# Forget gates' running sums: from 8 partitions x 1024 tokens to 128 partitions x 64 tokens

## The chip, the core and the metric

The kernel runs on one core of a Trainium2 chip. The core has five engines that each work through a queue of their own in order: TensorE (PE, with weight loads shown as PEld), VectorE (DVE), ScalarE (ACT), GpSimd (POOL) and SyncE (SP), which here only starts DMA transfers. ACT and POOL start transfers too. The engines wait for each other by semaphores. The metric is the device time of one execution in microseconds (us), as the median of several runs.

## The reference

One layer of a hybrid encoder: a normalisation, one wide projection, two kinds of attention, an output projection, and a feed-forward part. The change is about one small piece, the forget gates of the first attention:

```
log_f = jax.nn.log_sigmoid((fa + forget_bias).astype(jnp.float32))   # 8 heads x 1024 tokens
c = jnp.cumsum(log_f, axis=-1)                                        # running sum over the tokens
sc = q k^T * scale + c[query] - c[key]                                # used as a bias of the scores
```

`fa` is eight columns of the projection (one per head). So of each head 1024 numbers are needed: z = fa + bias, log sigmoid(z) = min(z, 0) - log(1 + exp(-|z|)), and the running sum of that over the tokens.

## The kernel before

The activations lie transposed, 1024 features on partitions by two halves (h = 0, 1) of 512 tokens. Matrix products are done in float32 quality with pairs of fp32r parts, a high part and a low part (`wh`, `wl` of a weight, `...h`, `...l` of an operand), three PE instructions for each. The projections use a Strassen scheme: a unit computes 2x2 blocks in seven products of 12 matmuls each, named here by their operands: B11, T2, T1, T3, B21, B22, T4. Four PSUM banks (`u_0` to `u_3`) belong to a unit. After a product DVE or ACT reads its bank (`p` on ACT L543; `u` L545, `c` L547 and L549, `cc` L557 on DVE), and the later products B22 and T4 add into banks 2 and 3 after `c` has read them. PSUM has two pools of four banks, `psd[0]` and `psd[1]`, which the units take in turn.

The order of work around the change is that of lines 608 to 616: `project_qk(0)`; then for each of four steps `project_v(i)`, `project_qk(i+1)` and `finish()`, which transposes the projected v through PE (`vtp`, L594) into banks of `psd[1]` and splits it (`vs`, L278; casts on ACT, subtractions on DVE). `forget()` is called once, behind the first of these steps. A scheduler of the framework sorts the recorded instructions into each engine's queue, by its own estimate of when each can start; so the instructions of `forget` are mixed into those of the second v unit and the second and third q/k units. POOL splits the weights (`wl`, L167, and the sums `S`); SP loads them (`wr`, L160, four buffers); ACT casts the high parts (`wh`, L165) and sends every output of a q/k unit with six DMA issues (L573, L574).

`forget` (L407) works in two halves of 512 tokens on 8 partitions, one per head. For each half it loads the raw columns from `c_dram` (where L385 had put them), multiplies by rstd, and does ten more DVE instructions and two ACT functions (Exp L418, Ln L420, each with a load of its table); the running sum is a scan (L428) that starts from the last value of the half before. The sums go back to `c_dram` (L432). They are read at the start of attention (`cr`, L438, and `bc`, L453).

Of the kernel before, what the change touches and what calls it, by code (L numbers as in the profile page):

```python
# [11 lines left out]
F32 = mybir.dt.float32  # L12
F32R = mybir.dt.float32r
AF = mybir.ActivationFunctionType
ALU = mybir.AluOpType
# [62 lines left out]
def hs(h):  # L78
    return slice(h * HALF, (h + 1) * HALF)
# [3 lines left out]
def hybrid_block(ctx: ExitStack, tc: tile.TileContext, xT, xN, g1, wall, wf, fb, relb, relt, rows, g2, g3, outT):  # L83
# [28 lines left out]
    def tmp(name, dt=F32):  # L112
        return tp.tile([P, HALF], dt, tag="t", name=name, bufs=8)
# [22 lines left out]

    cpool.tile([P, 24], F32, tag="gap", name="gap")
    rstd = cpool.tile([P, S], F32, tag="rstd", name="rstd")
# [268 lines left out]
    def forget():  # L407
        bt = cpool.tile([NH, 1], F32, tag="fbt", name="fbt")
        load(bt, fb)
        last = 0.0  # L410
        for h in range(2):
            z = tmp("fz")[0:NH, :]
            load(z, c_dram[:, hs(h)])
            e, u, l = [tmp(f"f{n}")[0:NH, :] for n in "eul"]
            V.tensor_tensor(z, z, rstd[0:NH, hs(h)], op=ALU.mult)
            V.tensor_scalar(z, z, bt, None, op0=ALU.add)
            V.scalar_tensor_tensor(e, z, -1.0, z, op0=ALU.mult, op1=ALU.max)
            A.activation(e, e, AF.Exp, scale=-1.0)  # L418
            V.tensor_scalar(u, e, 1.0, None, op0=ALU.add)
            A.activation(l, u, AF.Ln)  # L420
            V.scalar_tensor_tensor(e, u, -1.0, e, op0=ALU.add, op1=ALU.subtract)
            V.reciprocal(u, u)
            V.tensor_tensor(e, e, u, op=ALU.mult)
            V.tensor_tensor(l, l, e, op=ALU.subtract)
            V.scalar_tensor_tensor(z, z, 0.0, l, op0=ALU.min, op1=ALU.subtract)
            V.memset(u, 1.0)
            c = e
            V.tensor_tensor_scan(c, u, z, last, ALU.mult, ALU.add)  # L428
            if h == 0:
                last = cpool.tile([NH, 1], F32, tag="clast", name="clast")  # L430
                V.tensor_copy(last, c[:, HALF - 1:HALF])
            store(c_dram[:, hs(h)], c)  # L432

# [673 lines left out]
def pack(inputs):  # L1107
# [26 lines left out]
    return {"xT": xT, "xN": xN, "g1": vec(a["norm1"][0]), "wall": np.ascontiguousarray(np.concatenate(wall)), "wf": wf,  # L1134
            "fb": np.ascontiguousarray(a["forget_bias"][0][:, None]),
            "relb": np.ascontiguousarray(a["rel_bias"][0][:, rel]),
# [19 lines left out]
```

## Time and profile before

| | |
|---|---|
| median of three runs | 1528.51 us (1525.95 to 1529.92) |
| the profiled execution, its own time | 1529.15 us |
| its span, first to last instruction | 1527.4 us |
| mean granted PE clock | 0.979 of full speed |
| PE busy | 1464.2 us, 96% of the span |
| DVE / ACT / POOL busy | 968.7 / 738.9 / 870.9 us |

The profile is one execution, recorded by the hardware. Starts and durations are in us from the span's start. Busy is time in which an instruction of the engine runs; idle time before an instruction is put down to the semaphore that came last. The share of a whole span is a mean over stages; what an edit is worth is read in its own stage, which here is the stretch from about 85 to 135 us.

### The profile page before, as it was taken

How to read it: one execution, taken by the hardware profiler on the slowest of the kernel's cores; microseconds unless marked ns; L12 is line 12 of the kernel's file. 1: busy time of each engine (PE TensorE's matmuls, PEld its weight loads, DVE VectorE, ACT ScalarE, POOL GpSimd, SP SyncE). 2: the span in 40 equal slices, each digit the busy share in tenths (PEclk: the TensorE clock that was granted, in tenths of full speed). 3: DMA queues.
4: the chain of work that ended last, by engine and by line, in shares of the span. 5: the costliest groups of instructions: out<-in, count | busy, mean ns of one | idle time of the engine just before them, and what ended most of it. 6: DMA issues, size and time to landing. Idle time of an engine off the chain costs nothing.

```text
span 1527.4 us, 20994 instructions
## 1 busy us (share of the span) xinstructions
PE 1464.2 (96%) x6772; PEld 1211.8 (79%) x6772; DVE 968.7 (63%) x1538; ACT 738.9 (48%) x1396; POOL 870.9 (57%) x705
## 2 busy tenths in 40 slices
PE   7998999999889899999999999999999899999996
PEld 5776888888778787888887888888888688888885
DVE  7777555644367677766424687666666447999543
ACT  8533333353348777667525543333333344444643
POOL 2468877778742222111086467888887445567462
PEclk9999999999989899999999999999999999999998
DMA  8536677773588787776466424444443856589363
GB/s 273 150 99 167 188 198 224 186 201 129 166 184 181 170 175 178 193 203 157 151 203 216 153 70 172 152 152 152 152 152 134 281 187 204 154 253 221 96 203 114
DMA packets 152623, 267.11 MB, mean 175 GB/s; under 512 B 22136, under 2 KB 39800, under 8 KB 149376
## 3 DMA queue, kind: packets, MB, share of 16 engines
q1 hardware_dynamic: 78272, 140.98, 30.2%
q10 hardware_dynamic: 50304, 84.24, 17.3%
q0 software_dynamic: 23936, 40.54, 12.4%
q8 instruction: 53, 0.87, 0.2%
q14 instruction: 58, 0.48, 0.1%
HBM read 179.38 MB, written 86.31 MB: 174 GB/s over the span
## 4 chain that ended last, share of the span: by engine, by line
PE 65%; DMA 10%; POOL 8%; DVE 7%; issue 6%; ACT 2%; ACTq 1%; SPq 0%; POOLq 0%; DVEq 0%
PE u L218 32%; PE dS L218 9%; PE dA L218 8%; PE o L218 4%; PE m L218 3%; DMA qk<-qk_dram 3%; POOL wl_S L167 3%; DMA rb<-r_dram 2%; PE pv L739 1%; PE s L489 1%; DMA wr<-wall 1%; PE pv L740 1%; PE pv L741 1%; PE st L724 1%; POOL wl_A L167 1%
## 5 line engine op out<-in xcount | busy, mean ns | idle before, releaser
L167 POOL TENSOR_TENSOR wl_A<-wr,wh_A 128x512 fp32r<-128x512 f32 x118 | 168.9, 1440 | 91.8 <-ACT wh_A L165 74.7
L167 POOL TENSOR_TENSOR wl_S<-S,wh_S 128x512 fp32r<-128x512 f32 x102 | 142.9, 1404 | 32.3 <-ACT wh_S L165 32.1
L278 DVE TENSOR_TENSOR tl<-p,th 128x512 fp32r<-128x512 f32 (+1 forms) x192 | 107.5, 580 | 31.7 <-ACT th L277 29.3
L165 ACT CAST wh_A<-wr 128x512 fp32r<-128x512 f32 x105 | 65.0, 620 | 98.2 <-DMA a_dram<-at 52.2
L165 ACT CAST wh_S<-S 128x512 fp32r<-128x512 f32 x105 | 64.0, 618 | 86.2 <-POOL S L190 35.7
L277 ACT CAST th<-p 128x512 fp32r<-128x512 f32 (+1 forms) x192 | 93.1, 508 | 12.5 <-PE pv L740 7.4
L167 POOL TENSOR_TENSOR wl_S<-ks,wh_S 128x512 fp32r<-128x512 f32 x48 | 68.1, 1446 | 52.6 <-ACT wh_S L96 50.7
L496 DVE CUSTOM_DVE_ANT_0 s<-s,bc 128x384 f32<-128x384 f32 (+3 forms) x128 | 69.8, 561 | 38.6 <-PE s L489 29.7
L557 DVE TENSOR_TENSOR cc<-u,u 128x512 f32<-128x512 f32 x70 | 48.1, 687 | 59.1 <-PE u L218 58.9
L489 PE MATMUL s<-qk 128*128 128x384 f32 (+2 forms) x192 | 65.2, 372 | 19.4 <-DMA qk<-qk_dram 10.8
L188 POOL TENSOR_TENSOR S<-wr,wr 128x512 f32<-128x512 f32 x35 | 49.4, 1410 | 53.9 <-DMA wr<-wall 40.2
L918 ACT ACTIVATE v<-v 128x512 f32<-128x512 f32 x64 | 40.5, 633 | 67.0 <-DVE v L917 67.0
L167 POOL TENSOR_TENSOR wl_A<-ka,wh_A 128x512 fp32r<-128x512 f32 x32 | 45.2, 1421 | 47.7 <-ACT wh_A L96 46.6
L739 PE MATMUL pv<-th,v 128*128 128x512 f32 (+1 forms) x192 | 66.1, 344 | 1.1 <-ACT on L752 0.9
L724 PE MATMUL st<-sk 82*128 82x512 f32 (+1 forms) x192 | 66.4, 346 | 0.5 <-DMA sk<-m_rows 0.5
L716 PE MATMUL st<-qk 128*128 128x512 f32 (+1 forms) x192 | 66.6, 349 | 0.0
L741 PE MATMUL pv<-tl,v 128*128 128x512 f32 (+1 forms) x192 | 65.9, 343 | 0.4 <-DVE tl L278 0.4
L740 PE MATMUL pv<-th,v 128*64 128x512 f32 (+1 forms) x192 | 65.4, 341 | 0.0
L277 ACT CAST qkh<-qk 128x512 fp32r<-128x512 f32 x32 | 19.9, 622 | 93.2 <-DMA qk_dram<-qkl 35.5
L736 ACT ACTIVATE p<-st,ncq 128x512 f32<-128x512 f32 (+1 forms) x96 | 54.6, 597 | 19.3 <-PE st L732 14.5
L489 PEld LDWEIGHTS s<-qk 128*128 128x128 f32 x192 | 37.3, 204 | 29.0 <-DMA qk<-qk_dram 12.5
L218 PE MATMUL u<-B11h,wh_A 128*128 128x512 f32 x140 | 55.4, 396 | 2.4 <-DVE vs L278 2.4
(397 smaller groups left out, 4986.8 us busy)
## 6 DMA issues: line engine op xcount, KB each, us to landing
wr<-wall SPq DMA_DIRECT2D x243, 256.0 KB
qk<-qk_dram POOLq DMA_DIRECT2D x16, 1024.0 KB, 6.4
a_dram<-at ACTq DMA_DIRECT2D x64, 256.0 KB
xT<-a_dram SPq DMA_DIRECT2D x64, 256.0 KB
qk_dram<-qkh ACTq DMA_DIRECT2D x96, 128.0 KB
a_dram<-v ACTq DMA_DIRECT2D x48, 256.0 KB
xB<-a_dram SPq DMA_DIRECT2D x44, 256.0 KB
z_dram<-zt ACTq DMA_DIRECT2D x32, 256.0 KB
```

The lines of the kernel that those rows point to most:

```text
L165: act.copy(wh, src)
L167: eng.tensor_tensor(wl, src, wh.bitcast(F32), op=ALU.subtract)
L218: eng.matmul(bank, w[wi], x[xi], start=(first and t == 0), stop=(t == n - 1 and not part), skip_group_check=part or not first)
L277: A.copy(dst[0], src)
L278: eng.tensor_tensor(dst[1], src, dst[0].bitcast(F32), op=ALU.subtract)
L489: T.matmul(ps[:, :n], qk[:, 1, i * P:(i + 1) * P], qk[:, 0, ks:ks + n], start=True, stop=not diag)
L496: V.tensor_tensor_reduce(ps[:, :v], ps[:, :v], bc[:, b0:b0 + v], 1.0, prev, ALU.add, ALU.min, out)
L716: T.matmul(ps[:, c], qk[:, 0, keys], qk[:, 1, qs], start=True, stop=False)
L724: T.matmul(ps[:, c], sk[:, 0, keys], sk[:, 1, qs], start=False, stop=not extra)
L739: T.matmul(pv[:, c], v3[hh][:, j, 1:3, :], th[:, c], start=first, stop=False)
L740: T.matmul(pv[0:HD, c], v3[hh][:, j, 0, :], th[:, c], start=False, stop=False)
L741: T.matmul(pv[:, c], v3[hh][:, j, 1:3, :], tl[:, c], start=False, stop=last)
```

## The change

`forget` now has two parts. First each half is loaded, multiplied by rstd on 8 partitions (`fr`), and stored back to `c_dram`. Then the whole is loaded again as 128 rows of 64 tokens: row 16 h + b holds block b of head h. Bias, log sigmoid and scan are done once on 128x64. What a block has to add from the blocks before it in its head is one float32 matmul (`fsum`): a 128x128 matrix of zeros and ones (`tri`, made by POOL) times the last column of the scanned blocks, into one column of a bank of `psd[1]`. It is added to every row, and the rows are stored. The bias comes as 128 values, each head's repeated 16 times. A padding tile grows from 24 to 32 columns.

```diff
     def forget():
-        bt = cpool.tile([NH, 1], F32, tag="fbt", name="fbt")
+        bt = cpool.tile([P, 1], F32, tag="fbt", name="fbt")
         load(bt, fb)
-        last = 0.0
         for h in range(2):
-            z = tmp("fz")[0:NH, :]
+            z = tmp("fr")[0:NH, :]
             load(z, c_dram[:, hs(h)])
-            e, u, l = [tmp(f"f{n}")[0:NH, :] for n in "eul"]
             V.tensor_tensor(z, z, rstd[0:NH, hs(h)], op=ALU.mult)
-            V.tensor_scalar(z, z, bt, None, op0=ALU.add)
...
-            V.memset(u, 1.0)
-            c = e
-            V.tensor_tensor_scan(c, u, z, last, ALU.mult, ALU.add)
-            if h == 0:
-                last = cpool.tile([NH, 1], F32, tag="clast", name="clast")
-                V.tensor_copy(last, c[:, HALF - 1:HALF])
-            store(c_dram[:, hs(h)], c)
+            store(c_dram[:, hs(h)], z)
+        before = tmp("tri")[:, 0:P].rearrange("p (h b) -> p h b", b=16)
+        G.memset(before, 1.0)
+        G.affine_select(out=before, in_=before, compare_op=ALU.is_ge, fill=0.0, base=-1,
+                        pattern=[[16, NH], [1, 16]], channel_multiplier=-1)
+        G.affine_select(out=before, in_=before, compare_op=ALU.is_ge, fill=0.0, base=0,
+                        pattern=[[-16, NH], [0, 16]], channel_multiplier=1)
+        c_rows = c_dram.rearrange("h (b j) -> (h b) j", j=64)
+        z, e, u, l = [tmp(f"f{n}")[:, 0:64] for n in "zeul"]
+        load(z, c_rows)
+        V.tensor_scalar(z, z, bt, None, op0=ALU.add)
+        V.scalar_tensor_tensor(e, z, -1.0, z, op0=ALU.mult, op1=ALU.max)
+        A.activation(e, e, AF.Exp, scale=-1.0)
+        V.tensor_scalar(u, e, 1.0, None, op0=ALU.add)
+        A.activation(l, u, AF.Ln)
+        V.scalar_tensor_tensor(e, u, -1.0, e, op0=ALU.add, op1=ALU.subtract)
+        V.reciprocal(u, u)
+        V.tensor_tensor(e, e, u, op=ALU.mult)
+        V.tensor_tensor(l, l, e, op=ALU.subtract)
+        V.scalar_tensor_tensor(z, z, 0.0, l, op0=ALU.min, op1=ALU.subtract)
+        V.memset(u, 1.0)
+        V.tensor_tensor_scan(e, u, z, 0.0, ALU.mult, ALU.add)
+        ps = psd[1].tile([P, HALF], F32, tag="d", name="fsum")
+        T.matmul(ps[:, 0:1], before.rearrange("p h b -> p (h b)"), e[:, 63:64], start=True, stop=True)
+        V.tensor_scalar(e, e, ps[:, 0:1], None, op0=ALU.add)
+        store(c_rows, e)
```

The scheduler's order changes only between about 60 us of the program and the end of the third q/k unit; behind it the queues read as before. On DVE, the queue from the end of the first v unit on: `u_943` and `c_944` are the evacuations of the second q/k unit, whose banks are `u_0_938` to `u_3_941`. Before:

```order
L585 TENSOR_TENSOR vt<-cc,rstd 128x512
L415 TENSOR_TENSOR fz<-fz,rstd 8x512
L416 TENSOR_SCALAR fz<-fz,fbt 8x512
L417 SCALAR_TENSOR_TENSOR fe<-fz 8x512
L545 TENSOR_TENSOR u_943<-u_1_939,p_942 128x512
L419 TENSOR_SCALAR fu<-fe 8x512
L421 SCALAR_TENSOR_TENSOR fe<-fu,fe 8x512
L422 RECIPROCAL fu<-fu 8x512
L547 TENSOR_TENSOR c_944<-u_2_940,u_943 128x512
L423 TENSOR_TENSOR fe<-fe,fu 8x512
L549 TENSOR_TENSOR c_944<-u_3_941,c_944 128x512
L424 TENSOR_TENSOR fl<-fl,fe 8x512
```

The same place on DVE now (lines behind `forget` are 9 higher: L547 is L556):

```order
L594 TENSOR_TENSOR vt<-cc,rstd 128x512
L414 TENSOR_TENSOR fr<-fr,rstd 8x512 x2
L554 TENSOR_TENSOR u_943<-u_1_939,p_942 128x512
L426 TENSOR_SCALAR fz<-fz,fbt 128x64
L427 SCALAR_TENSOR_TENSOR fe<-fz 128x64
L556 TENSOR_TENSOR c_944<-u_2_940,u_943 128x512
L429 TENSOR_SCALAR fu<-fe 128x64
L431 SCALAR_TENSOR_TENSOR fe<-fu,fe 128x64
L558 TENSOR_TENSOR c_944<-u_3_941,c_944 128x512
L576 SCALAR_TENSOR_TENSOR qk<-c_944,rstd 128x512
L278 TENSOR_TENSOR qkl<-qk,qkh 128x512
L576 SCALAR_TENSOR_TENSOR qk<-u_0_938,rstd 128x512
```

Both multiplies stand together in front of `u_943`, and `fz` with `fe`, which need the second load, stand in front of the first `c_944`; the reciprocal has moved behind the unit's four outputs.

On SP, the loads around `forget`; `wr` are weight quarters. Before:

```order
L160 DMA wr_2_1183<-wall 128x512
L413 DMA fz<-c_dram 8x512
L160 DMA wr_1_1185<-wall 128x512
L160 DMA wr_0_1328<-wall 128x512
L413 DMA fz<-c_dram 8x512
L160 DMA wr_3_1330<-wall 128x512
```

Now on SP:

```order
L160 DMA wr_2_1176<-wall 128x512
L413 DMA fr<-c_dram 8x512 x2
L425 DMA fz<-c_dram 128x64
L160 DMA wr_1_1178<-wall 128x512
L160 DMA wr_0_1321<-wall 128x512
L160 DMA wr_3_1323<-wall 128x512
```

The three loads of `forget` stand together; the last of them waits for the two stores, with the next weight quarter behind it.

On PE, the end of the second v unit (its product T4) and the start of the third q/k unit (B11 into `u_0`). Before:

```order
L218 MATMUL u_3_1224<-T4h,wh_A_1217 128x512
L218 MATMUL u_3_1224<-T4l,wh_A_1217 128x512
L218 MATMUL u_3_1224<-T4h,wl_A_1219 128x512
L218 MATMUL u_0_1370<-B11h,wh_A_1336 128x512
L218 MATMUL u_0_1370<-B11l,wh_A_1336 128x512
```

Now on PE:

```order
L218 MATMUL u_3_1217<-T4h,wh_A_1210 128x512
L218 MATMUL u_3_1217<-T4l,wh_A_1210 128x512
L218 MATMUL u_3_1217<-T4h,wl_A_1212 128x512
L439 MATMUL fsum<-fe,tri 128x1
L218 MATMUL u_0_1363<-B11h,wh_A_1329 128x512
L218 MATMUL u_0_1363<-B11l,wh_A_1329 128x512
```

`fsum` has come between them. Further up on PE, the first transposes `vtp` and eight matmuls of the second v unit's B11, which stood between B21 and B22 of the second q/k unit, now stand behind its T4.

## Rows read from the trace of the kernel before

**Rows 1.** The page, part 1: busy us, share of the span, instructions.

```profile
PE 1464.2 (96%) x6772; PEld 1211.8 (79%) x6772; DVE 968.7 (63%) x1538; ACT 738.9 (48%) x1396; POOL 870.9 (57%) x705
```

**Rows 2.** Waits of PE, 95 to 135 us: total us, times, longest.

```profile
PE u L218 <- DVE c L547: 2.6, 2, 1.4
PE u L218 <- DVE vs L278: 2.4, 1, 2.4
PE vtp L594 <- DVE cc L557: 1.1, 1, 1.1
PE u L218 <- POOL wl_A L167: 1.0, 1, 1.0
PE u L218 <- DVE c L549: 0.8, 1, 0.8
```

**Rows 3.** Waits of PE, 135 to 420 us.

```profile
PE s L489 <- DMA qk<-qk_dram: 4.8, 1, 4.8
```

**Rows 4.** Busy time by stretch: PE, PEld, DVE, ACT, POOL, clock, DMA.

```profile
95.00:135.00 40.00, 32.21 (x143) 24.27 (x141) 38.25 (x45) 16.30 (x28) 27.20 (x19) 1.00 0.54 136
```

**Rows 5.** Groups of DVE instructions, 85 to 135 us: busy us, mean ns.

```profile
L422 DVE RECIPROCAL fu<-fu 8x512 f32<-8x512 f32 x2 | 6.7, 3341 | 1.2 <-ACT fl L420 1.1
...
L421 DVE SCALAR_TENSOR_TENSOR fe<-fu,fe 8x512 f32<-8x512 f32 x2 | 3.4, 1717 | 0.0
...
L423 DVE TENSOR_TENSOR fe<-fe,fu 8x512 f32<-8x512 f32 x2 | 3.1, 1545 | 0.0
```

**Rows 6.** Timeline of PE: start, us, instruction, [idle before and releaser].

```profile
95.98 0.40 PE L218 MATMUL u<-B21h,wl_A 128*128 128x512 f32 x1
96.22 0.60 PE L594 MATMUL vtp<-ident,vt 128*128 128x128 f32 x4
96.57 0.48 PE L218 MATMUL u<-B11h,wh_A 128*128 128x512 f32 x1
...
101.10 0.50 PE L218 MATMUL u<-B22h,wh_S 128*128 128x512 f32 x1 [1.19 <-DVE c L547]
...
132.33 0.50 PE L218 MATMUL u<-B11h,wh_A 128*128 128x512 f32 x1 [2.39 <-DVE vs L278]
```

**Rows 7.** Timeline of SP's queue and of DVE at the first load.

```profile
87.49 0.32 SPq L413 DMA_DIRECT2D fz<-c_dram  x1
...
90.08 0.68 DVE L415 TENSOR_TENSOR fz<-fz,rstd 8x512 f32<-8x512 f32 x1 [4.16 <-DMA fz<-c_dram]
```

**Rows 8.** Small DVE instructions: a group, and ns min/median/max of one line.

```profile
L441 DVE TENSOR_SCALAR ncq<-cqt 128x64 f32<-128x64 f32 x1 | 0.2, 225 | 0.4 <-PE cqt L440 0.4
...
L240 DVE TENSOR_TENSOR n_t<-n_r x4: 161/438/1322, 902.0 to 1515.4; 128x4 f32<-128x4 f32 x4
```

**Rows 9.** Small transfers: chain of waits (start, us), and a load's timeline.

```profile
130.34 1.48 DMA c_dram<-fe
752.56 2.02 DMA r_dram<-d
...
590.95 0.37 SPq L759 DMA_DIRECT2D d<-d_dram  x1
593.91 0.25 DVE L761 RECIPROCAL d<-d 128x16 f32<-128x16 f32 x1 [0.92 <-DMA d<-d_dram]
```

**Rows 10.** Groups on POOL (a mask) and PE (one column).

```profile
L127 POOL TENSOR_SCALAR_AFFINE_SELECT raw<-raw 128x128 f32<-128x128 f32 x2 | 0.5, 287 | 0.0
...
L265 PE MATMUL n_s<-ones,rstd 128*128 128x1 f32 x32 | 4.7, 259 | 2.2 <-DVE rstd L234 2.2
```

**Rows 11.** Timeline of ACT: first and last of four casts of the second q/k unit's outputs.

```profile
105.40 0.62 ACT L277 CAST qkh<-qk 128x512 fp32r<-128x512 f32 x1 [7.31 <-DVE qk L567]
...
120.22 0.62 ACT L277 CAST qkh<-qk 128x512 fp32r<-128x512 f32 x1 [1.14 <-issue]
```

**Rows 12.** Busy time at 400 us; and a load's median us to landing.

```profile
400.00:440.00 40.00, 33.04 (x132) 25.79 (x130) 22.58 (x51) 10.63 (x19) 31.91 (x31) 0.89 1.02 236
...
sk<-sk_dram POOLq DMA_DIRECT2D x16, 512.0 KB, 8.6
```

More of the change, by code (lines that the diff above doesn't have):

```diff
@@ L135, in hybrid_block @@
     load(gt[:, 0, :], g1)
-    cpool.tile([P, 24], F32, tag="gap", name="gap")
+    cpool.tile([P, 32], F32, tag="gap", name="gap")
     rstd = cpool.tile([P, S], F32, tag="rstd", name="rstd")
@@ L407, in forget @@
     def forget():
-        bt = cpool.tile([NH, 1], F32, tag="fbt", name="fbt")
+        bt = cpool.tile([P, 1], F32, tag="fbt", name="fbt")
         load(bt, fb)
-        last = 0.0
         for h in range(2):
-            z = tmp("fz")[0:NH, :]
+            z = tmp("fr")[0:NH, :]
             load(z, c_dram[:, hs(h)])
-            e, u, l = [tmp(f"f{n}")[0:NH, :] for n in "eul"]
             V.tensor_tensor(z, z, rstd[0:NH, hs(h)], op=ALU.mult)
-            V.tensor_scalar(z, z, bt, None, op0=ALU.add)
[L417 to L425, printed above, removed]
-            V.memset(u, 1.0)
-            c = e
-            V.tensor_tensor_scan(c, u, z, last, ALU.mult, ALU.add)
-            if h == 0:
-                last = cpool.tile([NH, 1], F32, tag="clast", name="clast")
-                V.tensor_copy(last, c[:, HALF - 1:HALF])
-            store(c_dram[:, hs(h)], c)
@@ L1134, in pack @@
     return {"xT": xT, "xN": xN, "g1": vec(a["norm1"][0]), "wall": np.ascontiguousarray(np.concatenate(wall)), "wf": wf,
-            "fb": np.ascontiguousarray(a["forget_bias"][0][:, None]),
+            "fb": np.repeat(a["forget_bias"][0], 16)[:, None],
             "relb": np.ascontiguousarray(a["rel_bias"][0][:, rel]),
```

## The prediction

> **What bounds the kernel now.** I read the page's busy shares first: TensorE (PE) is busy for 1464.2 of 1527.4 us [rows 1], so an edit to the forget gates, which have hardly any PE work, can pay only where PE waits for them. The waits of PE, asked for stretch by stretch, put that place between 95 and 135 us: PE waits 7.9 us there in six waits (2.6 + 2.4 + 1.1 + 1.0 + 0.8), and all but 1.0 us of it is for VectorE (DVE) [rows 2]. From 135 to 420 us it has one wait of more than 1 us, 4.8 us for the first attention operands [rows 3]; so what is gained before 135 us moves everything up to there by as much. In the same 40 us DVE is busy for 38.25 us [rows 4]. The groups of instructions say with what: three lines of `forget` alone, of its twelve, take 13.2 us (6.7 + 3.4 + 3.1) [rows 5]. A reader should see in these rows that 8 partitions cost what 128 would: L421 on 8x512 takes 1.7 us, the reciprocal 3.3 us. DVE runs in order, so the evacuations of the projection's banks (`c`, L547 and L549, and `cc`, L557) stand behind these instructions, and PE's next products into the same banks stand behind the evacuations. The timeline of PE shows the first such wait at 101.10 us and the last at 132.33 us [rows 6].
>
> **What a wait costs.** A matmul's modelled end is 0.40 us after its start, while the next starts 0.24 us after it [rows 6], so each wait costs PE 0.16 us more than its idle column says. The six waits are worth 7.9 + 6 x 0.16 = 8.9 us from start to start. That is the most the change can give here.
>
> **The change, part by part.**
> *DVE.* The 8x512 work of lines 416 to 431 goes; two 8x512 multiplies by rstd stay, at 0.7 us each (90.08 [rows 7]). Eleven 128x64 instructions come. The nearest row is a 128x64 tensor_scalar of 0.23 us [rows 8]; I take 0.2 us for each, and 0.3 to 0.5 us for reciprocal and scan (3341 ns on 512 columns [rows 5], an eighth of it is 0.42). That is about 4 us of DVE where three lines alone took 13, and half the table loads of ScalarE (ACT).
>
> *The new round trip through DRAM.* This is what the change adds to the path. The order now puts, on DVE: both multiplies, `u`, then `fz` (the 128x64 add), `fe`, and only then `c` (L547 before, L556 now). `fz` waits for load, multiply, store, and load again, and everything on DVE waits behind it. The first load is issued at 87.49 us as before, and the first multiply starts at 90.08 [rows 7]; the second follows at once, so both are done at 91.5. Bounds of the store: 1.48 us (the c_dram store of before) and 2.02 us (the r_dram store). Bounds of the load: 2.6 us (87.49 to 90.08) and 3.0 us (590.95 to 593.91) [rows 7, 9]. So the data of `fz` are there at 95.6 to 96.5, and with two instructions of 0.2 us and `c` of 0.7 us, `c` is ready at 96.7 to 97.6. PE has finished the product B21 at 96.2 (last start 95.98 [rows 6]) and now goes straight to B22, which needs `c`: a wait of 0.5 to 1.4 us, and up to 1.1 us more if one of the three small instructions is held as long as L421 was over its shortest sister (1.72 against 0.67 us [rows 5, 7]). I take 1.3 us, in the middle.
>
> A 128x4 tensor_tensor of before took 0.16 us at the least and 1.32 us at the most [rows 8], so small DVE instructions are not always short. The Trainium skill, page "SBUF — State Buffer", section "Who interferes with whom", says why: a DVE instruction with two SBUF inputs and a GpSimd instruction that reads SBUF exclude each other for the whole instruction. By that rule it is the count of such instructions, not their columns, that is paid for, and held at 1.3 us in place of 0.2 for each of the multiply and `fe` the sum below would be 2.2 us worse. No row at 128x64 shows it yet.
>
> *POOL* builds the triangle: a memset and two affine_selects, 0.29 us each on 128x128 [rows 10]; I take the same for the memset. They stand between weight splits at 88 to 97 us, of which PE uses none before 103 us; the split that PE waited 1.0 us for [rows 2] is now needed after T4, at 103, so that wait goes. If the cover were gone they would cost 0.9 us.
>
> *ACT* waits at its head for the two multiplies (until 91.5) before it can send the stores; behind them stands the first weight cast of the next unit, whose product is now needed at 103.
>
> *PE* gains `fsum`. The nearest row is a float32 matmul of one column, 0.26 us [rows 10]. It stands behind T4 of the unit, which itself needs a `c` that DVE does after the scan; so `fsum` waits for nothing of the chain, and costs its 0.26 us.
>
> *SP.* The 128x64 load waits at the head of the queue for the two stores, to about 93.5. The weight load behind it stands there some 6 us longer than the first load of before, and the quarter that it brings is used by POOL after 100 us. I count nothing; if that cover is gone, POOL and PE are late by as much as the round trip.
>
> **What is late next.** With DVE free, ACT paces the stretch: each output of the q/k unit takes a cast and six DMA issues, and of the four casts `qkh` the first comes at 105.40 and the last at 120.22 [rows 11], 4.9 us apart in the mean. B22, which waits for the same evacuations, started at 101.10 [rows 6] and would now start at 97.5; so the four come some 3.7 us sooner, the fourth at 116.5. The second unit's `c` stands behind the fourth `qkl` (0.6 + 0.7 us later, then 0.7 of its own): 118.5. PE, with seven products of 12 x 0.23 us, four groups of transposes of 0.35 us (96.22 to 96.57 [rows 6]) and the first wait, gets there at 96.2 + 1.3 + 19.3 + 1.4 = 118.2: a wait of 0.3 us. Two products and `fsum` later it is at 124.3. The next unit's first bank is now that of the second transpose and not the first (the pool has four banks, and `fsum` takes the first), so it needs four of the eight `vs` casts: the first at about 121, a spacing behind the fourth `qkh`, the fourth `vs` some 5 us later with three weight casts and two pairs between, 125.7. That wait is 1.4 us.
>
> **The sum.** 8.9 us go. New are 1.3 + 0.3 + 1.4 us, with 0.16 each for the ends 3.5 us at most, and 0.3 for `fsum`: 5.1 us gained. The walk says the same from the other side: the product that started at 132.33 starts at about 125.8, a gain of 6.5 us. I take 6.0. The profiled execution took 1529.15 us, with 1.75 us around its span; it would become 1523.1. It lies 0.6 us above the median of the runs, 1528.51, so the median becomes 1522.5. With the ends of the round trip, of the held instructions and of the `vs` wait (none, to the 2.4 us of before) the gain lies between 2.5 and 8.9 us: 1519.6 to 1526.0.
>
> **The rivals.**
> *ACT paces it already* (its own waits are DMA issues and casts, [rows 11]): then the second and third new waits keep the size of the old ones (1.4 and 0.8 at the second v unit's B22 and T4, 2.4 at the bank), and what goes is the POOL wait and those of 1.2 [rows 6] and 1.1 us [rows 2], 3.8 with 0.16 each, less 1.3 for the round trip: about 2.5 us, 1526.0. Against it: the casts at 105.40 and 120.22 themselves come behind DVE's reciprocals.
> *It is given back later.* PE waits 4.8 us for the first attention load near 405 us, in a stretch where the DMA engines are full (share 1.02) [rows 3, 12]. If that load came no sooner, PE would wait up to 6 us longer there: 1528.5. Against it: the load is issued when buffers of the projections come free, which move with PE.
> *Slower: the round trip.* DVE stands still until the second load is there, with PE behind it. It decides from the point where B22's wait reaches 8.9 - 1.7 = 7.2 us, data at 102.3, which is 10.8 us after the multiplies; my bounds are 4.1 to 5.0. Were each leg as long as the 8.6 us that loads of sk take on POOL's queue [rows 12], the data would come at 108.7, the wait would be 13.6, and the kernel 6.4 us slower: 1534.9. For it speaks that both loads share SP's queue with 256 KB weight loads; against it, that the load of before had one just ahead and took 2.6 us.
>
> **How the numbers follow.** Forecast 0.62, ACT 0.17, given back 0.10, slower 0.11. A change of 0.3%, 4.6 us, is about what can be told from none. Of the forecast some nine tenths lie beyond a gain of 4.6 us: faster 0.56. The rest of it with the two rivals of little gain: same 0.33. Slower 0.11. The range for 8 in 10 takes in the forecast's own, with 1 us below it for the spread of the runs, and most of the two that lose the gain: 1518.5 to 1528.7.
>
> **What would show it.** Right: DVE's busy time from 95 to 135 us falls from 38.25 us by some 20; `fz` on 128x64 starts at 95.5 to 97; B22 starts at 97 to 98.5; the first product of the third q/k unit starts near 126 in place of 132.33; PE then runs without a wait up to about 400 us. Wrong: `fz` after 100 us; that product later than 130; or the wait near 400 us grown by what was gained.

## The result, and the profile after

| | before | changed |
|---|---|---|
| median of 15 runs each | 1531.99 us (1525.95 to 1543.15) | 1521.96 us (1513.19 to 1527.55) |
| ratio, 95% interval | | 0.9931 (0.9909 to 0.9954) |
| the profiled execution (span) | 1529.15 us (1527.4) | 1524.15 us (1522.4) |
| median of more runs | 1528.6 us (74, beside the experiments) | 1520.8 us (33 of three copies, the 15 above among them) |

The change is faster: the interval of the ratio lies below 1. How much it gains is known only roughly: the interval means 7 to 14 us of 1532, the first 15 runs of each kernel show 10 us, and 74 and 33 runs show 7.7. The forecast was a gain of 6.0 us from a median of 1528.51, to 1522.5.

Waits of PE in the changed kernel, 84 to 425 us (what it waited for; us in total, times, the longest):

```profile
PE s L498 <- DMA qk<-qk_dram: 5.1, 1, 5.1
PE u L218 <- DVE c L556: 1.8, 2, 1.0
PE u L218 <- DVE vs L278: 1.0, 1, 1.0
```

Six waits of 7.9 us [rows 2] have become three of 2.8; the wait for the first attention operands was 4.8 us [rows 3] and is 5.1. The same stretch as in [rows 4], in the changed kernel:

```profile
95.00:135.00 40.00, 37.20 (x170) 29.79 (x169) 26.74 (x41) 16.52 (x32) 27.53 (x21) 1.00 0.70 183
```

DVE (the third busy time) is down from 38.25 to 26.74 us, PE (the first) up from 32.21 to 37.20. The places of [rows 6], on PE's timeline of the changed kernel (start, us, instruction, [idle before and releaser]):

```profile
96.36 0.39 PE L218 MATMUL u<-B21h,wl_A 128*128 128x512 f32 x1
97.70 0.50 PE L218 MATMUL u<-B22h,wh_S 128*128 128x512 f32 x1 [0.96 <-DVE c L556]
...
119.97 0.50 PE L218 MATMUL u<-B22h,wh_S 128*128 128x512 f32 x1 [0.82 <-DVE c L556]
125.55 0.28 PE L439 MATMUL fsum<-fe,tri 128*128 128x1 f32 x2
126.84 0.50 PE L218 MATMUL u<-B11h,wh_A 128*128 128x512 f32 x1 [1.02 <-DVE vs L278]
...
408.05 0.58 PE L498 MATMUL s<-qk 128*128 128x256 f32 x1 [5.07 <-DMA qk<-qk_dram]
```

The first product of the third q/k unit, at 132.33 us before, starts at 126.84. I call it the mark. The last matmul of B21, where the prediction's walk begins, starts at 95.98 before and at 96.36 here; counted from it the mark comes 5.9 us sooner. The first attention matmul `s` started at 414.62 us in the kernel before and starts at 408.05 here: 6.6 us. (Of the 1.1 us between the two, 0.7 is one wait of before for ACT's `p` at 321.54, which the changed kernel does not have.) Now the chain that the change added, on DVE, with the POOL instructions beside it:

```profile
90.47 1.28 DVE L414 TENSOR_TENSOR fr<-fr,rstd 8x512 f32<-8x512 f32 x2 [3.89 <-DMA fr<-c_dram]
...
95.20 0.56 DVE L426 TENSOR_SCALAR fz<-fz,fbt 128x64 f32<-128x64 f32 x1 [2.85 <-DMA fz<-c_dram]
...
95.68 1.28 POOL L205 TENSOR_TENSOR wr<-wr,wr 128x512 f32<-128x512 f32 x1
...
95.80 1.25 DVE L427 SCALAR_TENSOR_TENSOR fe<-fz 128x64 f32<-128x64 f32 x1
...
96.97 0.68 DVE L556 TENSOR_TENSOR c<-u,u 128x512 f32<-128x512 f32 x1
...
98.47 2.54 POOL L167 TENSOR_TENSOR wl_S<-S,wh_S 128x512 fp32r<-128x512 f32 x2
98.59 1.25 DVE L431 SCALAR_TENSOR_TENSOR fe<-fu,fe 128x64 f32<-128x64 f32 x1
...
113.48 0.22 DVE L433 TENSOR_TENSOR fe<-fe,fu 128x64 f32<-128x64 f32 x1
...
114.98 1.29 POOL L188 TENSOR_TENSOR S<-wr,wr 128x512 f32<-128x512 f32 x1 [4.49 <-DMA wr<-wall]
```

The second load is there at 95.20 us, and `c`, on which B22 waits, can start only at 96.97, since `fe` takes 1.25 us beside a POOL instruction of 1.28 that began 0.12 us earlier. Later, with POOL idle for the 4.49 us before 114.98, five other 128x64 instructions take 0.11 to 0.29 us (one is shown), and the reciprocal 0.55. The wait for `vs` at the mark ends with the fourth of the eight `vs` subtractions; the second and the fourth:

```profile
124.23 0.42 DVE L278 TENSOR_TENSOR vs<-vtp,vs 128x256 fp32r<-128x256 f32 x1 [0.81 <-ACT vs L277]
...
126.38 0.41 DVE L278 TENSOR_TENSOR vs<-vtp,vs 128x256 fp32r<-128x256 f32 x1
```

The fourth ends at 126.79, and the mark starts at 126.84. ACT's first and fourth cast of [rows 11], now:

```profile
101.59 0.62 ACT L277 CAST qkh<-qk 128x512 fp32r<-128x512 f32 x1 [3.15 <-DVE qk L576]
...
117.62 0.62 ACT L277 CAST qkh<-qk 128x512 fp32r<-128x512 f32 x1 [3.24 <-DMA qk_dram<-qkl]
```

They come 3.8 and 2.6 us sooner. What the experiments had to settle: was the old loss DVE's work, or ACT's; what the three waits that are left consist of; and why medians and profiles do not show the same gain.

### The profile page after: what moved, and what is told of

Read it like the earlier page. It is cut to its first block, busy times and chain, and to the rows that moved or that the text cites. A ratio compares the mean times of both kernels' runs of the same rounds, so it can differ in the third digit from the quotient of the medians.

```text
span 1522.4 us, 20991 instructions
## 1 busy us (share of the span) xinstructions
PE 1462.8 (96%) x6774; PEld 1212.7 (80%) x6774; DVE 950.0 (62%) x1528; ACT 733.9 (48%) x1392; POOL 869.1 (57%) x708
## 4 chain that ended last, share of the span: by engine, by line
PE 73%; DMA 10%; DVE 6%; POOL 5%; issue 4%; ACT 2%; SPq 0%; ACTq 0%; DVEq 0%; POOLq 0%
PE u L218 36%; PE dS L218 11%; PE dA L218 8%; PE o L218 4%; DMA qk<-qk_dram 3%; PE m L218 2%; DMA wr<-wall 2%; DMA rb<-r_dram 2%; PE pv L748 2%; PE s L498 2%; PE pv L749 1%; PE pv L750 1%; PE st L725 1%; PE st L733 1%; PE dA L96 1%
## 5 line engine op out<-in xcount | busy, mean ns | idle before, releaser
L218 PE MATMUL u<-B21h,wh_A 128*128 128x512 f32 x140 | 55.7, 398 | 1.3 <-ACT p L552 1.3
```

What stands on the lines that cost most here:

```text
L218: eng.matmul(bank, w[wi], x[xi], start=(first and t == 0), stop=(t == n - 1 and not part), skip_group_check=part or not first)
```

## The experiments

All runs, with the mark and the first `s` from each profile. The third column is the time from the start of B21's last matmul to the mark; it leaves out what a profile was early or late ahead of the change (up to 1.2 us).

| kernel | mark us | from B21 us | first `s` us | median us (runs) | ratio to before, 95% |
|---|---|---|---|---|---|
| before | 132.33 | 36.35 | 414.62 | 1528.6 (74) | |
| changed | 126.84 | 30.48 | 408.05 | 1521.96 (15) | 0.9931 (0.9909 to 0.9954) |
| e1_again | 127.14 | 30.27 | 409.14 | 1519.56 (12) | 0.9936 (0.9912 to 0.9959) |
| e8_rot2 | 126.56 | 30.41 | 408.16 | 1521.85 (6) | 0.9942 (0.9919 to 0.9965) |
| e3_dve_cut | 122.47 | 26.57 | 402.98 | 1518.43 (12) | 0.9941 (0.9915 to 0.9967) |
| e9_wide_late | 123.81 | 26.59 | 417.83 | 1526.85 (12) | 0.9991 (0.9972 to 1.001) |
| e2_no_trip | 125.94 | 29.56 | 410.00 | 1518.86 (9) | 0.9926 (0.9894 to 0.9958) |
| e5_two_trips | 128.28 | 31.67 | 409.60 | 1524.12 (12) | 0.9962 (0.9935 to 0.999) |
| e5_three_trips | 124.53 | 28.69 | 407.42 | 1519.07 (12) | 0.9938 (0.9918 to 0.9959) |
| e7_neg | 127.23 | 30.46 | 408.58 | 1518.39 (12) | 0.9946 (0.9921 to 0.9972) |
| e6_psd0 | 135.79 | 39.12 | 419.75 | 1540.3 (8) | 1.0078 (1.0052 to 1.0105) |
| e4_split1 | 122.54 | 26.56 | 403.81 | 1516.1 (6) | 0.9914 (0.9884 to 0.9944) |
| e4_split1_again | 122.72 | 26.57 | 404.15 | 1514.73 (6) | 0.9908 (0.9888 to 0.9928) |
| e10_late | 123.23 | 26.58 | 406.34 | 1516.07 (6) | 0.9916 (0.9893 to 0.9939) |

**How far two profiles of one program differ (e1_again).** No edit.

> The changed kernel once more, to learn how far two profiles of one program lie apart: its profile was 5.0 us shorter than that of before, but the medians of 15 runs stand 10 us apart (1531.99 and 1521.96). Theory: up to the first attention operands PE's times repeat within 0.3 us (first product of the third q/k unit at 126.5 to 127.2 us); behind them, where the granted clock falls to its lower level in short pieces, two profiles of one program differ by several us; median ratio to before 0.991 to 0.997. Rival: the profile tells the whole gain; ratio 0.9967, within 0.001. Second rival: the work behind 420 us is steadily shorter in the changed kernel, by 4 to 5 us beside the 5.5 of the stretch from 95 to 135; then the second profile shows it at the same waits as the first.

The second profile repeats the first within 0.3 us at the mark (127.14), but only within 1.1 us at `s` (409.14), where the wait itself is 5.85 and not 5.07 us. Its whole span is 1514.4 us, 8.0 us shorter. Windows of the first profile, and then of the second; the third column from the right is the granted clock:

```profile
520.00:580.00 60.00, 55.63 (x325) 48.95 (x324) 44.21 (x130) 44.73 (x104) 17.14 (x24) 0.91 0.78 173
580.00:640.00 60.00, 56.05 (x302) 46.94 (x302) 44.50 (x116) 41.06 (x84) 11.93 (x15) 0.97 0.81 187
```

```profile
520.00:580.00 60.00, 56.16 (x346) 49.51 (x345) 48.02 (x137) 46.69 (x110) 17.36 (x24) 0.97 0.83 187
580.00:640.00 60.00, 58.02 (x317) 48.49 (x316) 47.21 (x125) 42.73 (x89) 12.04 (x16) 1.00 0.79 199
```

The same program executed 36 more matmuls in these 120 us (663 against 627 recorded), at granted clocks of 0.97 and 1.00 instead of 0.91 and 0.97. The third copy of the program (e8_rot2, below) has the high clocks of the second profile in these windows, 0.97 and 1.00, and yet the span of the first, 1522.4: it had fallen behind from 420 to 520 us, with 481 matmuls at a granted clock of 0.88 where the other two have 512 and 514 at 0.91. So the difference between profiles arises in the attention stretch behind `s`, at no fixed place in it. Over whole runs the time goes with the mean clock in both kernels: 15 runs of before with a mean clock of 0.983 or more have a median of 1524.4 us, 20 runs at 0.979 or less 1532.2; for the changed kernel it is 1515.2 (6 runs) and 1524.2 (7). Which of the two leads, clock or waits, this does not show. The 5.0 us between the first two profiles and the 10 us between the first medians can both be such draws. The theory held (ratio 0.9936), but for the 0.3 us, which it missed at `s`. The second rival (steadily less work behind 420 us) fell: from the first `s` to the end the kernel before takes 1112.8 us, the three copies 1114.4, 1105.3 and 1114.2.

**DVE's work alone (e3_dve_cut).** The kernel before, in `forget`:

```
 V.tensor_tensor(z, z, rstd[0:NH, hs(h)], op=ALU.mult)
-... ten DVE instructions on 8x512, Exp and Ln between them ...
+A.activation(e, z, AF.Exp, scale=-1.0)
+A.activation(l, e, AF.Ln)
+c = z
 ... the 8x1 copy ...
 store(c_dram[:, hs(h)], c)
```

> The kernel before, on 8 partitions with two loads and two stores, with all of forget's DVE work left out but the two multiplies and the 8x1 copy; ACT keeps its two Exp and two Ln with their table loads, whose results nothing reads. Theory (PE's waits between 95 and 135 us are DVE's 8x512 work): the waits of 7.9 us in six fall to 2 us or less, the first product of the third q/k unit starts at 125 to 127 us instead of 132.33, and the time is that of the changed kernel within 2 us. Rival (ACT's table loads, casts and DMA issues pace the stretch): the waits stay at 4 us or more and that product starts at 129 to 132.

The window and the two casts of ACT in this kernel:

```profile
95.00:135.00 40.00, 40.00 (x186) 33.21 (x185) 19.92 (x31) 15.29 (x31) 30.73 (x23) 1.00 0.69 187
```

```profile
98.05 0.62 ACT L277 CAST qkh<-qk 128x512 fp32r<-128x512 f32 x1
...
111.76 0.62 ACT L277 CAST qkh<-qk 128x512 fp32r<-128x512 f32 x1 [2.63 <-DMA qk_dram<-qkl]
```

PE is busy for all 40 us and has no wait at all, with ACT's four table loads in place. The casts, at 105.40 and 120.22 before [rows 11], come at 98.05 and 111.76: they followed DVE. The rival that ACT paces the stretch has fallen. The mark at 122.47, sooner than the 125 to 127 that I expected, is also the floor: four kernels below have the same 26.6 us from B21. The old `forget` cost 9.8 us by that count (9.9 at the mark), and the changed kernel still pays 3.7 to 3.9 of it. (Its end is no better than that of the changed kernel in the medians; see what stays open, below.)

**Place or width (e9_wide_late).** The kernel before with its 8x512 work one projection later:

```
-        if i == 0:
+        if i == 1:
             forget()
```

> The kernel before with its forget, 8 partitions and 512 columns, called one projection later; nothing else is changed. Theory (the cost is the 8x512 work itself, which makes DVE late wherever a projection runs beside it): PE's waits between 95 and 125 us fall to 1 us or less and come back between 125 and 175 us with 5 to 9 us in all; within 3 us of before at 240 us. Rival (the place is what costs, and the partitions matter little): 6 us or more ahead of before at 240 us, as the changed kernel is or better.

Stretch by stretch:

```profile
95.00:135.00 40.00, 40.00 (x186) 33.19 (x185) 25.40 (x34) 16.31 (x31) 32.19 (x23) 1.00 0.71 191
135.00:175.00 40.00, 33.12 (x143) 24.94 (x142) 36.71 (x42) 15.82 (x28) 27.34 (x19) 0.98 0.53 133
```

PE's waits move out of the first stretch into the second, 7.0 us in seven waits (0.6 of it for ACT's `p`, the rest for DVE), the last one again for `vs` with 2.4 us. The first `s` is at 417.83, 3.2 us later than before: 1.2 us were there ahead of the change (B21's last matmul starts at 97.22), and behind the last wait the granted clock is 0.50 from 174 to 176 us. The ratio is 0.9991. The 8x512 work takes its waits along wherever it goes; for this work the place alone gains nothing.

**The round trip taken away (e2_no_trip).**

```
-for h in range(2):
-    ... load, multiply by rstd, store ...
 load(z, c_rows)
```

> The changed kernel without its round trip: the 128x64 tile is loaded straight from the raw rows, and the multiplication by rstd with its two loads, two multiplies and two stores is left out. Theory (the trip costs the wait of B22 for c, 0.96 us idle, and no more): B22 starts at 96.5 to 97.0 us instead of 97.70, the first product of the third q/k unit at 125.5 to 126.2 instead of 126.84, 1 us less in all (ratio to before 0.992 to 0.993). Rival (ACT's head wait for the multiplies, 4.88 us before the first weight cast, delays the casts): the qkh casts come 2 us or more sooner and the gain is 2 to 3 us. Rival (the trip is fully covered): times as in the changed kernel within 0.3 us.

DVE, one POOL instruction and PE in this kernel:

```profile
92.03 1.22 DVE L420 TENSOR_SCALAR fz<-fz,fbt 128x64 f32<-128x64 f32 x1 [6.27 <-DMA fz<-c_dram]
93.29 0.24 DVE L421 SCALAR_TENSOR_TENSOR fe<-fz 128x64 f32<-128x64 f32 x1
93.86 0.94 DVE L423 TENSOR_SCALAR fu<-fe 128x64 f32<-128x64 f32 x1 [0.32 <-ACT fe L422]
94.71 1.29 POOL L190 TENSOR_TENSOR S<-S,wr 128x512 f32<-128x512 f32 x1
94.83 1.25 DVE L425 SCALAR_TENSOR_TENSOR fe<-fu,fe 128x64 f32<-128x64 f32 x1
...
96.78 0.69 DVE L550 TENSOR_TENSOR c<-u,u 128x512 f32<-128x512 f32 x1
...
97.53 0.50 PE L218 MATMUL u<-B22h,wh_S 128*128 128x512 f32 x1 [0.76 <-DVE c L550]
```

The mark came as expected (125.94), but not for the reason given: B22 starts at 97.53, not at 96.5 to 97.0, and still waits 0.76 us for `c`. With the data earlier, the order puts four small instructions ahead of `u` and `c` in place of two, and three of the four take 0.94 to 1.25 us. What went is the second unit's wait for `c` (0.82 us), while the one for `vs` grew from 1.02 to 1.64. The `qkh` casts came 2.2 to 3.6 us sooner, as the first rival had it, but the mark gained 0.9 us and not 2 to 3. One wait of 2.3 us for ACT's `p` at 316.38 then puts the first `s` at 410.00, behind that of the changed kernel. So taking the trip away did not free B22. Its wait came from what of `forget` stands ahead of `c`.

**A longer trip (e5_two_trips, e5_three_trips).**

```
 load(z, c_rows)
+store(c_rows, z)      # once, or twice
+load(z, c_rows)
```

> The changed kernel with its 128x64 tile stored to DRAM and loaded once more before use, so that fz has its data about 4.4 us later (99.3 to 100 us instead of 95.2). In the new order fz stands behind the first c of the q/k unit and before its second, so B22 no longer waits and T4 does. Theory (a DVE instruction at the head of its queue holds back the evacuation behind it, and PE with it, us for us once the cover is gone): B22 at 96.5 to 97.0, a wait of 1.5 to 3 us for the second c before T4, the first product of the third q/k unit 1 to 2 us later than 126.84. Rival (there is room for the trip): no wait of more than 0.5 us for c, and that product at 126 or sooner.

> The changed kernel with two more trips through DRAM for its 128x64 tile (three in all), so that the data of fz come at 104 to 106 us. The order now puts fz behind both c, two qk and a qkl, ahead of the first cc. Theory (what costs is what stands behind the waiting instruction, not the length of the trip): no wait for c at B22 or T4, the first transposes at 102.5 to 103 us; cc stands behind fz until 105 to 107, which delays the casts of qkh after the second, and the first product of the third q/k unit starts at 126.5 to 129. Rival (every microsecond that the data come later costs one, as from one trip to two: 1.1 to 1.4 us later for 4.4): that product at 129.5 or later.

With two trips, DVE and then PE:

```profile
99.60 0.36 DVE L428 TENSOR_SCALAR fz<-fz,fbt 128x64 f32<-128x64 f32 x1 [6.28 <-DMA fz<-c_dram]
100.00 1.22 DVE L429 SCALAR_TENSOR_TENSOR fe<-fz 128x64 f32<-128x64 f32 x1
101.14 0.68 DVE L560 TENSOR_TENSOR c<-u,c 128x512 f32<-128x512 f32 x1
...
101.87 0.50 PE L218 MATMUL u<-T4h,wh_A 128*128 128x512 f32 x1 [2.15 <-DVE c L560]
```

As the theory had it: no wait at B22, 2.15 us at T4, the mark 1.4 us later than in the changed kernel. But the waits do not explain the 1.4 us: up to the mark they sum to 2.95 us here (2.15 and 0.80 for `vs`) and to 2.80 there, since the second unit's wait for `c` is gone. What is new is the clock behind the 2.15 us (the third column from the right):

```profile
103.00:106.00 3.00, 3.00 (x9) 2.35 (x8) 2.42 (x6) 0.62 (x1) 0.00 (x0) 0.50 0.39 82
```

PE is at the lower of its two levels there, and from 102.93 to 105.92 its matmuls start 0.43 us apart in place of 0.23: seven times 0.2, about 1.4 us. So the second trip cost what the theory said, in good part by another way than it said.

With three trips the data come at 103.7 us, and both `c` stand ahead of `fz`. DVE, and the POOL instruction that follows:

```profile
103.69 0.26 DVE L430 TENSOR_SCALAR fz<-fz,fbt 128x64 f32<-128x64 f32 x1 [1.90 <-DMA fz<-c_dram]
103.98 0.23 DVE L431 SCALAR_TENSOR_TENSOR fe<-fz 128x64 f32<-128x64 f32 x1
...
106.98 1.29 POOL L167 TENSOR_TENSOR wl_S<-wr,wh_S 128x512 fp32r<-128x512 f32 x1 [4.65 <-ACT wh_S L165]
```

PE has one wait up to the mark, 1.6 us for `cc`, and the mark is at 124.53: 2.3 us sooner than in the changed kernel (1.8 counted from B21), with two trips more. I had expected 126.5 to 129: what the theory said of `c` held, its time for the mark did not. Here the longer trip costs less, since the order puts `fz` behind what PE needs; and `fz` and `fe` then meet an idle POOL and take 0.26 and 0.23 us instead of 0.56 and 1.25.

**One operand in place of two (e7_neg).**

```
-V.scalar_tensor_tensor(e, z, -1.0, z, op0=ALU.mult, op1=ALU.max)
+V.tensor_scalar(e, z, -1.0, None, op0=ALU.mult)
```

> The changed kernel with fe, the second 128x64 instruction of DVE, made from one SBUF operand (times -1) instead of two (the larger of z and -z); the absolute value is left out. The order of all queues is the same. Theory (fe took 1.25 us because it reads two operands from SBUF while a POOL instruction reads SBUF, and waited for POOL's end): fe takes 0.2 to 0.6 us, B22 starts at 96.7 to 97.1 instead of 97.70 with 0.3 us of wait or none, the first product of the third q/k unit 0.5 to 1 us sooner. Rival (the duration is that of a 128x64 instruction behind another, whatever it reads): fe takes 1.0 to 1.3 us and nothing else moves.

```profile
95.78 1.30 POOL L205 TENSOR_TENSOR wr<-wr,wr 128x512 f32<-128x512 f32 x1
...
95.92 1.22 DVE L427 TENSOR_SCALAR fe<-fz 128x64 f32<-128x64 f32 x1
```

My theory fell: with one operand from SBUF `fe` takes 1.22 us as well. But the rival (this is simply its duration) falls too, with the 0.23 us beside an idle POOL above. In all pairs shown, the long ones end within 0.1 us of the POOL instruction beside them (95.92 + 1.22 against 95.78 + 1.30; 95.80 + 1.25 against 95.68 + 1.28; in e2_no_trip 94.83 + 1.25 against 94.71 + 1.29). So it is POOL's instruction that sets the end, with one operand as with two. The Trainium skill, page "SBUF — State Buffer", section "Who interferes with whom", has this case in another sentence than the one I drew on: a tensor_scalar can run in a mode that takes both port pairs, and then excludes GpSimd as well. The rows agree; no run here shows which mode it ran in.

**The bank of fsum (e6_psd0, e8_rot2).**

```
-ps = psd[1].tile([P, HALF], F32, tag="d", name="fsum")
+ps = psd[0].tile([P, HALF], F32, tag="d", name="fsum")      # e6_psd0
```

```
 ps = psd[1].tile([P, HALF], F32, tag="d", name="fsum")
+psd[1].tile([P, HALF], F32, tag="d", name="turn")           # e8_rot2
```

> The changed kernel with fsum in a bank of the other PSUM pool, all else as it is. Theory (the vs wait of 1.0 us comes from fsum taking a bank of the third q/k unit's pool, so that the unit begins in the bank of the second transposes and not of the first): the wait goes, the first product of the third q/k unit starts at 125.6 to 126.1 us instead of 126.84 or 127.14. Rival (the casts of vs come too late for either bank): the wait stays at 0.8 us or more. Rival (the bank is then missing in the other pool): a new wait of 1 us or more for an evacuation in the unit behind, 135 to 180 us.

> The changed kernel with one more bank taken from fsum's pool and never used, so that the third q/k unit begins in the bank of the third transposes and not of the second; all queues keep their order. Theory (the vs wait of 1.0 us is the bank that the unit begins in): the wait grows by the spacing of the vs pairs, 1.7 to 2.5 us, to 2.5 to 3.7 us, and the first product of that unit starts at 128.4 to 129.6 us. Rival (that product waits for something else, and the bank is chance): a wait of 0.8 to 1.3 us, as before, at 126.5 to 127.3.

Neither moved the bank as it was meant to. In e8_rot2 the mark, 126.56, again follows the fourth `vs`, which ends at 126.50; one bank further would have meant the sixth, at 128.95. PE's order is that of the changed kernel, its three waits are 0.71, 0.94 and 1.01 us: a bank that nothing writes cost no turn, and the run is a third copy of that kernel. In e6_psd0 the order moved `fsum` on PE, to ahead of the whole next unit:

```profile
114.36 0.56 PE L439 MATMUL fsum<-fe,tri 128*128 128x1 f32 x2 [5.83 <-DVE fe L437]
114.78 0.77 PE L218 MATMUL u<-B11h,wh_A 128*128 128x512 f32 x1
115.35 0.63 PE L218 MATMUL u<-B11l,wh_A 128*128 128x512 f32 x1
115.78 0.63 PE L218 MATMUL u<-B11h,wl_A 128*128 128x512 f32 x1
...
118.76 0.39 PE L218 MATMUL u<-B11h,wh_A 128*128 128x512 f32 x1
```

Here PE stands 5.83 us for the scan, and 3.1 us for a `cc` before it. And behind that wait nine matmuls take some 0.43 us each from start to start instead of 0.23 (114.78 to 118.76). The granted clock was down all that time, from behind the wait for `cc`:

```profile
109.00:118.00 9.00, 3.64 (x10) 2.99 (x11) 5.29 (x9) 3.29 (x5) 4.04 (x4) 0.50 0.79 209
```

That is the lower of TensorE's two levels; from 119 us on it is 1.00 again. The kernel is slower than before (1.0078), but the order of the attention matmuls changed as well, so how much of that is `fsum`'s is not shown. By its timeline the run shows what the one new matmul costs if it stands where its operand is late. In the changed kernel it stands at 125.55, 11 us behind the scan.

**The later part one projection later (e4_split1, twice), and the whole (e10_late).**

```
 def forget():
     ... multiply by rstd, store ...
+def forget_sums():
     ... the bias, the triangle, everything from the 128x64 load on ...
         if i == 0:
             forget()
+        if i == 1:
+            forget_sums()
```

> The changed kernel with forget cut in two: the two multiplies by rstd and their stores stay where they are, everything from the 128x64 load on is issued one projection later (behind the third q/k unit and the second finish of v). The load's data are then long there when fz comes to the head of DVE's queue. Theory (the two c waits, 1.8 us, are fz and the small instructions held beside it; the vs wait, 1.0 us, is the bank that fsum takes): all three go, the first product of the third q/k unit starts at 124.3 to 125.5 us instead of 126.84, no new wait of over 0.7 us comes behind it, and at 300 us PE is 7.5 to 9 us ahead of before (the changed kernel: 5.8 and 5.5 in two profiles). Rival (the small instructions cost the same wherever they stand between POOL's splits): new waits for c or vs of 1.5 us or more between 135 and 180 us, and 5.5 to 6.5 us ahead at 300 us.

> The kernel of e4_split1 once more, since its first interval (0.9884 to 0.9944) overlaps that of the changed kernel. Theory (its 9.9 us at 240 us are the c and vs waits that went, and stay): 9.6 to 10.3 us ahead of before at 240 us, no wait of PE of over 0.7 us between 95 and 400 us, ratio to before 0.989 to 0.993. Rival (the first runs were lucky in the stretch behind 420 us, and its gain over the changed kernel is lost there): ratio 0.993 to 0.997.

> The changed kernel with forget called whole, round trip and all, one projection later (behind the third q/k unit). Theory (what e4_split1 gained over the changed kernel is the trip out of DVE's queue): fz stands ahead of the first c of that unit and waits for the second load; PE waits 1 to 3 us for c between 130 and 160 us, and is 7 to 9 us ahead of before at 240 us (changed kernel 5.8, e4_split1 9.9). Rival (the later place is all): no wait of over 0.7 us, 9.5 to 10.3 us ahead at 240 us.

The two stretches in e4_split1:

```profile
95.00:135.00 40.00, 40.00 (x186) 33.04 (x185) 23.06 (x35) 14.96 (x30) 33.64 (x27) 1.00 0.70 192
135.00:175.00 40.00, 40.00 (x187) 33.21 (x186) 27.98 (x38) 16.10 (x32) 32.58 (x25) 1.00 0.65 185
```

PE has no wait from 84 us to the first `s`; the mark is at 122.54 and 122.72, at the floor and sooner than I expected, and `s` at 403.81 and 404.15, 10.5 to 10.8 us sooner than before. The medians, 1516.1 and 1514.73 us, give the lowest two ratios here (0.9914 and 0.9908; e10_late has 0.9916); the intervals still overlap with the changed kernel's (0.9909 to 0.9954), so that it beats the changed kernel up to the first `s` is shown by PE's timeline, and only made likely for the whole by the medians. The instructions of `forget` are the same in number. I had expected their data to be there long before; they are not, and `fz` still stands at the head of DVE's queue for its load.

```profile
129.21 0.81 DVE L426 TENSOR_SCALAR fz<-fz,fbt 128x64 f32<-128x64 f32 x1 [1.92 <-DMA fz<-c_dram]
```

But it and three more small instructions are done by 131.14, around the start of the next unit's `u` at 131.05, and no product of PE waits behind them; three later ones that take 1.2 to 1.28 us beside POOL cost PE nothing either. `fsum` takes a bank there too, without a wait for `vs`. The whole of `forget` moved, with its trip, has one wait left:

```profile
165.00 0.50 PE L218 MATMUL u<-B11h,wh_A 128*128 128x512 f32 x1 [1.35 <-DVE vs L278]
```

I had expected waits for `c` there; there are none, though `fz` waits 4.43 us for its load. `s` is at 406.34, 2.2 to 2.5 us later than with the split; 0.5 to 0.7 us of that was there ahead of the change (B21's last matmul starts at 96.65, in the split at 95.98 and 96.15), and the rest is this wait, at the mark's place one projection on.

The wait for `vs` takes two things together. The bank decides which `vs` the unit needs: the mark starts 0.05 to 0.06 us behind the end of the second `vs` in the kernel before (132.28, without `fsum`), and behind that of the fourth in the three copies of the changed kernel. In the changed kernel the second `vs` ends at 124.65, before PE is through with T4 and `fsum` at 125.82, so with that bank there would be no wait at these times (no run tried it). And DVE decides when the fourth comes: in the split it ends at 162.49, ahead of PE, in e10_late, where the trip had held DVE earlier in the unit, at 164.94, and PE waits.

## Why the prediction was right

*The bound and the cause* were right. The waits were DVE's 8x512 work: without it they are gone (e3_dve_cut), and one projection later they come again (e9_wide_late). The 8.9 us put on them were a little low: the floor says 9.8 us. Part of this is the price of a wait beyond its idle time, put at 0.16 us: the first matmul behind a wait also holds the next one, which starts 0.34 us after it (101.10 and 101.44 in the kernel before) and not 0.23, another 0.1 us for each of six.

*The new waits* were 3.0 us by the prediction and are 2.8, 2.5 and 2.7 in three profiles. B22 had 1.3 and shows 0.96, 0.81 and 0.71; the second unit's had 0.3 and shows 0.82, 0.70 and 0.94; `vs` had 1.4 and shows 1.02, 1.03 and 1.01. The places are right and the sum is close, but no single term is: two were put too high and one too low, and that they nearly cancel is luck. The second load's data were to come at 95.6 to 96.5 us and came at 95.20. The wait for `vs` came as it was argued: the unit needs the fourth.

*The sum*: a gain of 5.1 us by the ledger, 6.5 by the walk, 6.0 taken. The mark moved by 5.5, 5.2 and 5.8 us in the three copies, and by 5.9, 6.1 and 5.9 counted from B21; the first `s` by 6.6, 5.5 and 6.5; the medians of all runs by 7.7. With the floor's 9.8 in place of 8.9 the ledger's 5.1 becomes 6.0, so the value taken between the two sums was near what the stretch gave. That the median of the first 15 runs, 1521.96, lies so close to 1522.5 is luck: in these runs the kernel before had 1531.99 and not 1528.51.

*Its steps that failed.* "I take 0.2 us for each" of the 128x64 instructions: two of those ahead of a `c` took 1.25 us beside POOL, as did the last one behind `fsum` (1.26), which is the end of the range that the prediction kept for held instructions. By the timeline, the 1.0 us that `fe` took beyond 0.23 is all of B22's 0.96 us; no run took it away alone (e7_neg was meant to). DVE's busy time was to fall by some 20 us from 95 to 135 us and fell by 11.5: work that had been pushed out of the full stretch came into it (eight `vs` subtractions instead of four), and the held instructions count as busy. The fourth cast was to come 3.7 us sooner and came 2.6 sooner, and the `qkl` behind it took 1.04 us and not 0.7; so the second unit's `c` was ready at 119.9 and not 118.5, PE was there at 119.15 and not 118.2, and the wait is 0.8 and not 0.3.

*The rivals.* ACT as the pace: fallen, by e3_dve_cut. Given back near 405 us: 0.2, 1.0 and 0.6 us of it in the three copies (4.84 before; 5.07, 5.85 and 5.46). Slower by the round trip: a load that comes late does hold PE through DVE (2.15 us at T4 with a second trip), but the other waits shrank by as much, and the time that this kernel lost came with a lower clock behind the wait; a third trip made PE's waits smaller, since the place in the queue moves with the length.

*What stays open.* From the first `s` on, gains are not carried to the end one for one. e3_dve_cut is 5 us ahead of the changed kernel there, and its interval (0.9915 to 0.9967) is no lower than the changed kernel's; those of e7_neg and e5_three_trips overlap with it too. The intervals are 6 to 8 us wide, so such a gain can be lost in them. From the first `s` to the end the profiles above, e6_psd0 apart, take 1105 to 1116 us. What decides the clock in the attention stretch was not tried.

## What to carry to other kernels

An instruction on 8 partitions cost what one on 128 did (0.64 us for `fr` on 8x512, 0.68 for `c` on 128x512); on an engine that evacuates PSUM for a full PE, folding rows into partitions paid here even at the price of a trip through DRAM. Then look at what stands ahead of an evacuation in that engine's queue: an instruction whose data are not there, or one that a neighbour engine holds, can cost PE as much as real work, and moving the later part to where no product waits behind it gave 4 us more at the first attention matmul. A profile of before and one of after tell where the time went; how much it is, in a kernel whose clock varies from run to run, only many runs tell.

## What the runs showed of the hardware that was not expected

- A 128x64 tensor_scalar, tensor_tensor or scalar_tensor_tensor of DVE takes 0.18 to 0.26 us beside an idle POOL and up to 1.26 us beside a 128x512 tensor_tensor of POOL, with one SBUF operand (1.22) as with two (1.25); it ends within 0.1 us of POOL's. A 128x64 memset, which reads nothing, takes 0.11 us in either case (149.50 in e4_split1, with POOL busy from 149.40 to 150.70).
- The clock can fall in the middle of a projection. In e6_psd0 the granted clock was 0.50 from 109 to 118 us, behind PE's wait of 3.11 us for `cc` and through most of that of 5.83, and matmuls then started 0.43 us apart in place of 0.23; in e5_two_trips it was 0.50 from 103 to 106 us, behind 2.15 us, in e9_wide_late from 174 to 176, behind 2.38 us. The wait alone does not decide it: the kernel before has 1.00 from 132 to 136 us, behind 2.39 us. In the changed kernel, with waits of up to 1.02 us, it stays 1.00 from 95 to 135.
- Two profiles of one program differ by 8.0 us in span (1522.4 and 1514.4), most of it from 520 to 640 us, where the granted clock was 0.91 and 0.97 in the one, 0.97 and 1.00 in the other; a third has the clocks of the second there and the span of the first.
